# Fewer waits on VectorE, and sixteen partitions of one load moved to GpSimd's queue

## The chip, the cores and the metric

One core of a Trainium2 chip runs the kernel. The metric is the device time of one execution in microseconds (us), the median of several runs. Runs of the kernel before lie within 0.3% of each other in most rounds (172.23 to 172.75 us) and within 0.6% in the worst. All runs used here are marked fast. "Chain" below means the chain of work that ended last, followed back from the last instruction. The profile is one traced execution; its span is about 2 us shorter than the device time (170.5 against 172.72 before).

## The reference

```python
x = np.abs(np.random.randn(32, 512, 1024)).astype(np.float32) + 1e-6
return np.sum(1.0 / x, axis=-1).astype(np.float32)
```

That is 16,384 rows of 1024 numbers, 67.1 MB in, 64 KB out. With 128 partitions, each partition holds 128 consecutive rows.

## The kernel before

It takes 1/a + 1/b = (a + b)/(ab) for the two halves of a row, so one reciprocal serves two numbers. GpSimd multiplies the halves (some rows: TensorE copies a half to PSUM and VectorE multiplies). ScalarE makes exp(-ln(ab)). Then VectorE multiplies and sums. "A" rows multiply both halves by the reciprocal; the rows of "B" and "C" take a + b from TensorE, and a C chunk leaves one of its products to VectorE.

```python
A, B, C = (2, 0, 0), (2, 2, 0), (2, 2, 1)      # rows, sums by TensorE, products by VectorE
LOADS = [[A, B, A, C]] * 10 + [[A, B], [A, C]] * 4 + [[A], [B], [A], [C]] * 2
...
ring = opool.tile([P, R, D], f32)              # R = 40 rows per partition
...
    for j in range(e, m):
        row = xc[:, j, :].rearrange("p (h e) -> p h e", h=2)
        sum_row(c + j, row, rc[:, j - e, :].unsqueeze(1).to_broadcast([P, 2, H]))
    for j in range(e):
        sum_row(c + j, pr[:, j, :], sm[j])
...
for chunks in LOADS:
    n = sum(m for m, _, _ in chunks)
    xt = ring[:, c0 % R : c0 % R + n, :]
    keep(nc.sync.dma_start(out=xt, in_=x_v[:, c0 : c0 + n, :]))
```

There are 26 loads: ten of 8 rows (numbers 0 to 9), eight of 4 (10 to 17), eight of 2. Up to 40 rows stand in the ring, so SyncE queues loads some 37 us before they land.

## Time and profile before

| | before |
|---|---|
| device time | 172.72 us (172.23 to 172.75, 3 runs) |
| span of the profile | 170.5 us |
| busy: PE, VectorE, ScalarE, GpSimd | 80, 73, 78, 78% |
| DMA over the span | 394 GB/s, 9 tenths or more in 36 slices |
| last load: first and last of its 16 landings | 158.94 and 162.02 us |

How to read it: no compute engine is full, the DMA engines are. A load's semaphore (the counter on which engines wait) counts 16 landings; the profile's busy share of the 16 DMA engines is 1.00 to 1.01 from 13 to 158 us. I read the landings as one from each engine; no trace names the engine. The prediction works out from this what sets the end.

### The profile page before, as it was taken

To read this page: it belongs to the slowest core of one execution; us is meant where nothing else is said; L and a number is where in the kernel's file an instruction comes from. 1 tells how busy PE (TensorE), PEld (TensorE's weight loads), DVE (VectorE), ACT (ScalarE), POOL (GpSimd) and SP (SyncE) were. 2 spreads that over 40 slices of the span, in tenths; PEclk is the share of its full clock that TensorE was granted. 3 is DMA by queue.
4 is the path that set the end of the run, shared out by engine and by line. 5 is a ranking of instruction groups with operands and counts; after the bars stand their busy time and mean duration, and the time that the engine had idled before them with its cause. 6 is when DMAs were issued, how large, how long until landed. Compare 5 with 4: busy or idle time off the path is not lost.

```text
span 170.5 us, 1320 instructions
## 1 busy us (share of the span) xinstructions
PE 136.0 (80%) x288; PEld 52.7 (31%) x288; DVE 124.9 (73%) x272; ACT 133.5 (78%) x129; POOL 133.0 (78%) x70
## 2 busy tenths in 40 slices
PE   0008999988889888786988887979999998896790
PEld 0003444332332333242333323323434332332240
DVE  0001778777987777787777769888998988889683
ACT  3002979979787997959799797899999988999790
POOL 1008969696996969589696969999999799996930
PEclk9999999999999999999999999999999999999999
DMA  6999999999999999999999999999999999999300
GB/s 208 415 446 431 438 423 446 415 454 423 448 423 431 431 438 419 431 432 423 446 415 446 423 404 427 431 423 431 427 427 423 427 413 423 421 421 419 146 0 15
DMA packets 3895, 67.25 MB, mean 394 GB/s; under 512 B 432, under 2 KB 560, under 8 KB 560
## 3 DMA queue, kind: packets, MB, share of 16 engines
q1 hardware_dynamic: 3888, 67.18, 92.7%
q8 instruction: 2, 0.03, 0.1%
q14 instruction: 5, 0.04, 0.1%
HBM read 67.11 MB, written 0.07 MB: 394 GB/s over the span
## 4 chain that ended last, share of the span: by engine, by line
DMA 66%; POOL 23%; issue 6%; DVE 1%; ACT 1%; DVEq 0%; POOLq 0%
DMA ring<-in_x_dram 66%; POOL pr L136 23%; DVE ring L92 1%; ACT pr L147 1%; ACT rc L151 1%; DVE pr L92 0%; DVEq L190 0%; POOLq L136 0%; DVE sums L92 0%; DVEq L92 0%
## 5 line engine op out<-in xcount | busy, mean ns | idle before, releaser
L136 POOL TENSOR_TENSOR pr<-ring 128x1024 f32<-128x1024 f32 x64 | 132.3, 2099 | 29.9 <-DMA ring<-in_x_dram 29.7
L82 PE MATMUL s<-ring,ident 128*128 128x512 f32 x256 | 121.2, 612 | 14.7 <-DVE sums L92 13.0
L92 DVE CUSTOM_DVE_ANT_1 ring<-ring,rc 128x1024 f32<-128x1024 f32 x64 | 75.6, 1219 | 26.2 <-ACT rc L151 22.2
L147 ACT ACTIVATE pr<-pr 128x1024 f32<-128x1024 f32 x64 | 67.3, 1051 | 30.0 <-POOL pr L136 29.7
L82 PEld LDWEIGHTS s<-ring,ident 128*128 128x128 f32 x256 | 47.4, 193 | 86.6 <-issue 49.4
L92 DVE CUSTOM_DVE_ANT_0 pr<-pr,s 128x512 f32<-128x512 f32 x64 | 41.4, 683 | 0.8 <-ACT pr L157 0.7
L157 ACT ACTIVATE pr<-pr 128x1024 f32<-128x1024 f32 x32 | 33.8, 1057 | 1.0
L151 ACT ACTIVATE rc<-pr 128x1024 f32<-128x1024 f32 x32 | 32.9, 1028 | 1.0
L82 PE MATMUL b<-ring,ident 128*128 128x512 f32 x32 | 18.5, 662 | 16.0 <-DMA ring<-in_x_dram 15.8
L125 DVE TENSOR_TENSOR pr<-ring,b 128x512 f32<-128x512 f32 x16 | 10.9, 684 | 16.1 <-PE b L82 16.0
L82 PEld LDWEIGHTS b<-ring,ident 128*128 128x128 f32 x32 | 5.3, 196 | 26.6 <-issue 15.4
L92 DVE DVE_READ_ACCUMULATOR2_ANT sums<- 128x1 f32 x128 | 10.6, 83 | 0.0
L53 ACT ACT_TABLE_LOAD x1 | 1.3, 1283 | 0.7 <-PEq L179 0.7
masks.py:197 POOL MEMSET ident<- 128x128 f32 x1 | 0.2, 204 | 0.3 <-POOLq L179 0.3
masks.py:199 POOL TENSOR_SCALAR_AFFINE_SELECT ident<-ident 128x128 f32<-128x128 f32 x1 | 0.3, 292 | 0.1
L179 POOL MEMSET const-float32-0.0<- 128x1 f32 x1 | 0.1, 98 | 0.2 <-issue 0.2
L179 POOL MEMSET const-bfloat16-1.0<- 128x1 bf16 x1 | 0.1, 101 | 0.0
L179 POOL MEMSET const-uint8-127<- 128x1 uint8 x1 | 0.1, 101 | 0.0
L179 POOL MEMSET const-float32-1.0<- 128x1 f32 x1 | 0.1, 98 | 0.0
## 6 DMA issues: line engine op xcount, KB each, us to landing
ring<-in_x_dram SPq DMA_DIRECT2D x10, 4096.0 KB, 37.7
ring<-in_x_dram SPq DMA_DIRECT2D x8, 2048.0 KB, 36.7
ring<-in_x_dram SPq DMA_DIRECT2D x8, 1024.0 KB, 28.2
out_dram<-sums SPq DMA_DIRECT2D x1, 64.0 KB, 1.5
```

Source lines behind the costliest of these rows:

```text
L53: nc.scalar.add_instruction(mybir.InstLoadActFuncSet(name=nc.get_next_instruction_name(), act_func_set_id=act_sets.index("natural_log_exp_ ...
L82: i = nc.tensor.matmul(bank, lhsT=ident, rhs=half, start=k == 0, stop=k == len(halves) - 1,)
L92: i = nc.vector.tensor_tensor_reduce(out=row, in0=row, in1=fac, scale=S, scalar=0.0, op0=mult, op1=plus, accum_out=sums[:, c : c + 1],)
L125: i = nc.vector.tensor_tensor(out=pr[:, j, :], in0=xt[:, q + j, :H], in1=b, op=mult)
L136: i = nc.gpsimd.tensor_tensor(out=pr[:, v:, :], in0=xc[:, v:, :H], in1=xc[:, v:, H:], op=mult)
L147: keep(nc.scalar.activation(out=pr, in_=pr, func=Ln, scale=S))
L151: i = nc.scalar.activation(out=rc, in_=pr[:, e:, :], func=Exp, scale=-1.0)
L157: keep(nc.scalar.activation(out=r, in_=r, func=Exp, scale=-1.0))
L179: nc = _bacc.Bacc("TRN2", target_bir_lowering=False, num_devices=1)
```

## The change

The intent, as I read it from the diff: VectorE's program becomes shorter (separate semaphore waits go from 87 to 51, and five C chunks become B), and the 16 DMA engines are to end together: in load 10 (rows 80 to 83), 16 of the 128 partitions are taken from SyncE's transfer and given to GpSimd's queue, in two groups of eight, each behind a transfer of eight single elements. The diff, cut to its core:

```diff
+    UPPER, Q, AHEAD = 80, 112, 64
-    LOADS = [[A, B, A, C]] * 10 + ...
+    LOADS = [[A, B, A, B], [A, B, A, C]] * 5 + ...
-    ppool: bufs=6, one tag
+    ppool: bufs=4 for each of two tags, "ps" and "pr"
     # sum_rows
+                pr[:, e : e + 2, :] if j == e and m - e > 1 else None,   # output of an A chunk's first row
-        for j in range(e):
+        for j in reversed(range(e)):
     # loads
-        keep(nc.sync.dma_start(out=xt, in_=x_v[:, c0 : c0 + n, :]))
+        if c0 == AHEAD:
+            for p0 in range(Q, P, 8):
+                for w, rows in ((1, 1), (D, 4)):
+                    dst = spare if rows == 1 else ring
+                    r0 = 0 if rows == 1 else UPPER % R
+                    keep(nc.gpsimd.dma_start(
+                        out=dst[p0 : p0 + 8, r0 : r0 + rows, :w],
+                        in_=x_v[p0 : p0 + 8, UPPER : UPPER + rows, :w]))
+        h = Q if c0 == UPPER else P
+        keep(nc.sync.dma_start(out=xt[:h], in_=x_v[:h, c0 : c0 + n, :]))
```

(The two ppool lines are paraphrased.)

More of the change, by code (lines that the diff above doesn't have):

```diff
@@ L41 @@
     A, B, C = (2, 0, 0), (2, 2, 0), (2, 2, 1)
-    LOADS = [[A, B, A, C]] * 10 + [[A, B], [A, C]] * 4 + [[A], [B], [A], [C]] * 2
+    LOADS = [[A, B, A, B], [A, B, A, C]] * 5 + [[A, B], [A, C]] * 4 + [[A], [B], [A], [C]] * 2
     Ln = mybir.ActivationFunctionType.Ln
@@ L60 @@
     )
-    ppool = ctx.enter_context(tc.tile_pool(name="ppool", bufs=6))
+    ppool = ctx.enter_context(tc.tile_pool(name="ppool", bufs=4))
     opool = ctx.enter_context(tc.tile_pool(name="opool", bufs=1))
@@ L75 @@
     sums = opool.tile([P, F], f32)
+    spare = opool.tile([P, 1, 1], f32)
     ident = opool.tile([P, P], f32)
@@ L89, in add, with sum_row @@
             keep(i)
-    def sum_row(c, row, fac):
+    def sum_row(c, row, fac, out=None):
         i = nc.vector.tensor_tensor_reduce(
-            out=row,
+            out=row if out is None else out,
             in0=row,
@@ L107, in sum_rows @@
             row = xc[:, j, :].rearrange("p (h e) -> p h e", h=2)
-            sum_row(c + j, row, rc[:, j - e, :].unsqueeze(1).to_broadcast([P, 2, H]))
-        for j in range(e):
+            sum_row(
+                c + j,
+                row,
+                rc[:, j - e, :].unsqueeze(1).to_broadcast([P, 2, H]),
+                pr[:, e : e + 2, :] if j == e and m - e > 1 else None,
+            )
+        for j in reversed(range(e)):
             sum_row(c + j, pr[:, j, :], sm[j])
@@ L116 @@
         xt = ring[:, c0 % R : c0 % R + n, :]
-        keep(nc.sync.dma_start(out=xt, in_=x_v[:, c0 : c0 + n, :]))
+        if c0 == AHEAD:
[3 more added lines that the diff above has]
+                    r0 = 0 if rows == 1 else UPPER % R
+                    keep(
+                        nc.gpsimd.dma_start(
+                            out=dst[p0 : p0 + 8, r0 : r0 + rows, :w],
+                            in_=x_v[p0 : p0 + 8, UPPER : UPPER + rows, :w],
+                        )
+                    )
+        h = Q if c0 == UPPER else P
+        keep(nc.sync.dma_start(out=xt[:h], in_=x_v[:h, c0 : c0 + n, :]))
         made, q = [], 0
         for m, e, v in chunks:
-            pr = ppool.tile([P, m, H], f32, tag="pr")
+            pr = ppool.tile([P, m, H], f32, tag="ps" if e else "pr")
             for j in range(v):
```

## The prediction

The forecast's sum came to -0.9 - 0.5 - 0.05 = -1.45 us, and the reason for the -0.5 us (on which engines the rows of load 10 land) is an assumption that was not shown. Without that term the sum is -0.95 us, 171.8 us. The sign "within 1.7 us" leans on the same term. Cut as well are an allowance for GpSimd's issues, which counted 0 us, and a fourth case: that the transfers of load 10 themselves run slowly, at 173.5 to 176 us, with the chance of 0.15 that is missing from the list; the 0.03 for over 2% slower is its worst part.

> **What bounds the kernel now.** I read first the slices of the page, because they show whether one resource is busy from end to end.
>
> ```profile
> DMA  6999999999999999999999999999999999999300
> GB/s 208 415 446 431 438 423 446 415 454 423 448 423 431 431 438 419 431 432 423 446 415 446 423 404 427 431 423 431 427 427 423 427 413 423 421 421 419 146 0 15
> q1 hardware_dynamic: 3888, 67.18, 92.7%
> q8 instruction: 2, 0.03, 0.1%
> q14 instruction: 5, 0.04, 0.1%
> ```
>
> The 16 DMA engines are full from the first slice to slice 37 and then stop. No compute engine is over 80% (PE 80, GpSimd and ScalarE 78, VectorE 73), so the middle of the kernel is a stream of 67.1 MB. The records of single packets give the rate: a row of 32 KB takes 1.213 us on its engine (27.0 GB/s), one of 16 KB 0.614 us, one of 8 KB 0.313 us. Each engine carries 1/16 = 4.19 MB, 155.3 us at that rate. It starts at 1.75 us, so an engine with nothing else to do would end near 157 to 158 us.
>
> Next the busy time by stretches, to see how the stream ends (us, then PE, PEld, DVE, ACT, POOL, clock, DMA share, GB/s):
>
> ```profile
> 156.00:158.00 2.00, 0.78 (x2) 0.49 (x3) 1.93 (x6) 1.97 (x3) 0.97 (x2) 1.00 1.01 422
> 158.00:159.00 1.00, 1.00 (x3) 0.38 (x2) 0.27 (x1) 0.60 (x1) 1.00 (x1) 1.00 0.77 320
> 159.00:160.00 1.00, 1.00 (x4) 0.51 (x3) 1.00 (x3) 0.35 (x1) 0.92 (x2) 1.00 0.24 98
> 160.00:161.00 1.00, 0.89 (x3) 0.06 (x1) 1.00 (x1) 0.97 (x2) 1.00 (x1) 1.00 0.16 66
> 161.00:162.00 1.00, 0.00 (x0) 0.00 (x0) 0.28 (x3) 0.79 (x1) 1.00 (x1) 1.00 0.02 8
> ```
>
> Most engines are done at 160 us; a few run on to 162. The semaphore of each load records 16 landings[...]. In the last load they lie at 0 to 1.00 us after the first for 13 engines, and at 2.17, 2.18 and 3.08 for three. The load is usable only at the last, 162.02 us. In the first load all 16 lie within 0.89 us, so the lag grows on the way, in steps: one engine 0.29 further at load 4, one to 2.15 at load 6, one to 2.2 at load 10, one to 2.17 at load 16, and one from 2.19 to 3.09 at load 23.
>
> These steps follow the instruction packets of q8 and q14, the only other traffic. Their records stand at 46.25, 73.07, 105.51, 106.37 and 154.09 us (8 KB each) and 64.89 and 131.32 (16 KB). Beside each, one data packet is too long: at 154.41 an 8 KB row took 0.968 us in place of 0.313. So the fetch at 154.09 costs its engine 0.327 + 0.655 = 0.98 us. I counted instructions in the trace: VectorE had started 69, 199 and 325 by 46.25, 105.51 and 154.09, steps of about 128. I read these three as VectorE's fetches, all on one DMA engine: 3 x 0.97 over a starting offset of 0.2 gives the 3.09 of the last engine.
>
> Last, the chain that ended last:
>
> ```profile
> 131.56 25.52 DMA ring<-in_x_dram
> 157.08 0.02 issue
> 157.11 0.04 POOLq L136
> 157.15 0.09 issue
> 157.24 2.36 POOL pr L136
> 159.60 0.09 issue
> 159.69 2.38 POOL pr L136
> 162.07 0.02 issue
> 162.09 1.07 ACT pr L147
> 163.16 0.02 issue
> 163.18 1.04 ACT rc L151
> ```
>
> Load 23's slowest landing (157.08) releases GpSimd, then come GpSimd's product for load 24 (which itself landed at 159.56), ScalarE, VectorE, and the store: 13.4 us from that landing to the end at 170.5. The end moves with the slowest DMA engine of the last three loads.
>
> [...]
>
> **The change, part by part.**
>
> *VectorE's program.* Three edits cut it: the first row of an A chunk writes to pr, the two rows of B and C are taken in reverse, and the tiles are split over two tags with four buffers each. From the built programs: VectorE has 364 instructions before and 323 after; 36 of the 41 are separate semaphore waits (87 to 51), 5 are products. The third fetch came at about the 325th traced instruction (327th of the program with its two branches). 323 stays below that, by four, so this fetch should not happen. The slowest engine then ends at 3.09 - 0.95 = about 2.15, beside the other two at 2.17 and 2.18: -0.9 us. The waits themselves are worth little: they lie beside the stream, and in the tail I see 0.04 + 0.09 us between ScalarE's end and the first VectorE row. I put 0.05 down for it.
>
> *Five C chunks become B.* Five VectorE products at 0.684 us (3.4 us) and ten TensorE passes go; GpSimd gains 5 half products of about 1 us. A load takes 9.71 us to arrive and costs GpSimd 7.4 us before, 8.4 in the five new ones. Both fit: 0 us.
>
> *Load 10 (rows 80 to 83).* SyncE's part has 112 partitions: 16 engines with 7 rows of 16 KB in place of 8, each 0.61 us less. The two GpSimd groups have 8 rows each. [...]
>
> *GpSimd's issues.* No duration of one is in this trace[...]. GpSimd has 2.3 us spare per load, and loads stand 36.5 us in the queue at the median, so no transfer should start late. 0 us.
>
> Sum if all works: -0.9 - 0.5 - 0.05 = -1.45 us, and 172.72 - 1.45 = 171.3 us. The tail moves as a whole, because load 22 (153.70) falls back by the 0.6 us that GpSimd needs to be free in time.
>
> **Rivals.**
>
> *Only the fetch counts.* [...] the move helps some and loads others: the last engine ends at 2.18 to 2.79 and the gain is 0.3 to 0.9 us, 171.8 to 172.4. For it: the trace names no engine.
>
> [...]
>
> *The fetch still comes*, if my boundary is off by four instructions or GpSimd's longer program (123 to 137) crosses one of its own: the -0.9 falls away and 172.1 to 172.7 remains. GpSimd fetched once, at its 68th; its next would be at about 196. Against.
>
> **Range and chances.** I give the full sum 0.55, the fetch alone 0.2, no gain 0.1[...]. The centre lies a little above the full sum: 171.5 us, range 170.7 to 173.6. Over 2% faster would be under 169.3 us, which needs 3.4 us from a spread of 3.1: 0.02. Over 2% slower is above 176.2[...]: 0.03. Within 2%: 0.95.
>
> **What would show it.** Right: four 8 KB instruction packets on q14 in place of five, none near 154 us; the last load's landings within 1.7 us; last landing near 160.5; the tail after load 23's landing still about 13.4 us. Wrong: long data packets between 95 and 120 us[...], a landing spread still above 2 us[...], a fifth packet (boundary), or SyncE's loads issued so late that DMA slices fall below 9.

## The result, and the profile after

The changed kernel takes 181.01 us (180.38 to 181.47, 4 runs) against 172.55 us for the kernel before beside it: ratio 1.049, 95% interval 1.045 to 1.053. It is slower by 8.5 us, where 171.5 was predicted. A ratio here is the mean time of one kernel's fast runs over that of the other's of the same rounds, so it is not quite the ratio of the medians.

The slices and queues of the changed kernel (each digit or number is 1/40 of the span, here 4.49 us):

```profile
DMA  6999999999999999999999899999999999999300
GB/s 219 438 424 438 438 438 409 453 431 402 440 446 424 424 453 427 418 431 438 416 431 415 194 161 234 299 431 422 431 427 427 427 414 418 425 418 425 166 0 15
q1 hardware_dynamic: 3872, 66.91, 92.0%
q0 software_dynamic: 128, 0.26, 0.9%
q8 instruction: 2, 0.03, 0.1%
q14 instruction: 4, 0.03, 0.0%
```

Two things are to be seen. The row of busy shares looks the same as before, one 8 among the nines: in the slow slices packets of 32 KB were open for up to 3.3 us in place of 1.21, and as I read it an engine counts as busy while a packet is open. The GB/s row beneath it does not: four slices show 194, 161, 234 and 299 in place of some 427. That is 233 + 266 + 193 + 128 = 820 GB/s missing, times 4.49 us 3.7 MB, or 8.6 us of the full rate: the whole loss. And q14 has four instruction packets in place of five, as predicted.

Stretches of the changed kernel (us, then PE, PEld, VectorE, ScalarE, GpSimd busy, granted clock, DMA share, GB/s):

```profile
95.00:98.00 3.00, 2.84 (x7) 1.40 (x8) 0.79 (x5) 2.08 (x2) 3.00 (x2) 1.00 1.10 418
98.00:102.00 4.00, 1.85 (x5) 0.53 (x4) 3.57 (x8) 3.67 (x4) 4.00 (x3) 0.96 0.91 180
...
104.00:108.00 4.00, 0.91 (x2) 0.50 (x2) 0.93 (x2) 0.88 (x1) 0.64 (x1) 0.50 0.98 156
108.00:112.00 4.00, 4.00 (x6) 1.65 (x5) 2.01 (x6) 2.08 (x2) 4.00 (x3) 0.51 1.03 238
112.00:115.00 3.00, 3.00 (x8) 1.32 (x8) 3.00 (x7) 2.71 (x3) 3.00 (x3) 1.00 0.93 229
115.00:118.00 3.00, 3.00 (x8) 1.33 (x8) 2.02 (x5) 2.94 (x4) 2.87 (x2) 1.00 1.01 431
```

The rate falls at 98 us, when GpSimd's first eight rows of 16 KB move (their packets start at 98.06 to 98.40, with one at 100.56), again with the second eight (104.25 to 107.65), and is back at 115 us, when load 10 and its neighbours are through. In between, 32 KB packets took up to 3.3 us in place of 1.21, GpSimd's sixteen rows 0.71 to 2.32 us, and most other 16 KB packets about 1.1 us, up to 2.6, in place of 0.614. TensorE's granted clock falls to 0.5 here too; it is not needed for the loss: the run with two halves below loses 6.5 us with a mean clock of 1.000.

The chain of the changed kernel, near its end:

```profile
135.94 27.02 DMA ring<-in_x_dram
...
163.08 2.37 POOL pr L157
...
165.60 2.35 POOL pr L157
...
168.05 2.38 POOL pr L157
170.43 0.02 issue
170.46 1.06 ACT pr L168
171.52 0.02 issue
171.55 1.04 ACT rc L172
```

The tail is nearly that of before. Here three products of GpSimd follow the landing of load 22 without a gap; before, GpSimd stood idle for 1.03 us in between, until load 23 landed (157.08). From the landing of load 22 (162.95) to the end are 16.6 us; before it was 153.70 to 170.5, 16.8 us. From the landing of load 23 (165.44), the sign that the prediction names, it is 14.0 us in place of 13.4. From the last landing of the last load to the landing of the output it is 7.66 us in place of 7.47, so only 0.2 us was lost there. The first landing of the last load moved from 158.94 to 167.25 and the last from 162.02 to 170.36. Note the first one: the DMA engine that fared best lost 8.3 us. No engine escaped. (Loads were queued long before, 38 us in the median, so late issue is no explanation.)

### The profile page after: what moved, and what is told of

It reads as the page before. It is cut to its first block, busy times and chain, and to the rows that moved or that the text cites. A ratio compares the mean times of both kernels' runs of the same rounds, so it can differ in the third digit from the quotient of the medians.

```text
span 179.5 us, 1277 instructions
## 1 busy us (share of the span) xinstructions
PE 137.3 (76%) x278; PEld 52.4 (29%) x278; DVE 122.5 (68%) x267; ACT 134.3 (75%) x129; POOL 140.6 (78%) x74
## 4 chain that ended last, share of the span: by engine, by line
DMA 79%; POOL 11%; DVE 3%; ACT 2%; issue 2%; SPq 0%; POOLq 0%; DVEq 0%
DMA ring<-in_x_dram 79%; POOL pr L157 11%; DVE pr L95 2%; DVE ring L95 1%; ACT pr L168 1%; ACT rc L172 1%; SPq L138 0%; POOLq L157 0%; DVE sums L95 0%; DVEq L95 0%; DVEq L211 0%
## 5 line engine op out<-in xcount | busy, mean ns | idle before, releaser
L157 POOL TENSOR_TENSOR pr<-ring 128x1024 f32<-128x1024 f32 x64 | 137.7, 2180 | 30.6 <-DMA ring<-in_x_dram 28.0
L85 PE MATMUL s<-ring,ident 128*128 128x512 f32 x256 | 126.4, 634 | 31.9 <-DVE sums L95 15.9
L85 PEld LDWEIGHTS s<-ring,ident 128*128 128x128 f32 x256 | 48.4, 198 | 106.6 <-issue 65.5
L95 DVE CUSTOM_DVE_ANT_1 pr<-ring,rc 128x1024 f32<-128x1024 f32 x32 | 39.1, 1221 | 48.4 <-ACT rc L172 48.2
L95 DVE CUSTOM_DVE_ANT_1 ring<-ring,rc 128x1024 f32<-128x1024 f32 x32 | 38.9, 1217 | 0.0
L85 PE MATMUL b<-ring,ident 128*128 128x512 f32 x22 | 13.3, 687 | 5.8 <-DMA ring<-in_x_dram 5.5
L146 DVE TENSOR_TENSOR pr<-ring,b 128x512 f32<-128x512 f32 x11 | 7.5, 684 | 5.2 <-PE b L85 5.1
L85 PEld LDWEIGHTS b<-ring,ident 128*128 128x128 f32 x22 | 4.0, 213 | 15.1 <-DMA ring<-in_x_dram 13.9
L132 POOL DMA_DIRECT2D spare<-in_x_dram x2 | 1.2, 610 | 0.0
L132 POOL DMA_DIRECT2D ring<-in_x_dram x2 | 1.0, 521 | 0.0
```

The source lines that it names most:

```text
L85: i = nc.tensor.matmul(bank, lhsT=ident, rhs=half, start=k == 0, stop=k == len(halves) - 1,)
L95: i = nc.vector.tensor_tensor_reduce(out=row if out is None else out, in0=row, in1=fac, scale=S, scalar=0.0, op0=mult, op1=plus, accum_out ...
L132: nc.gpsimd.dma_start(out=dst[p0 : p0 + 8, r0 : r0 + rows, :w], in_=x_v[p0 : p0 + 8, UPPER : UPPER + rows, :w],)
L146: i = nc.vector.tensor_tensor(out=pr[:, j, :], in0=xt[:, q + j, :H], in1=b, op=mult)
L157: i = nc.gpsimd.tensor_tensor(out=pr[:, v:, :], in0=xc[:, v:, :H], in1=xc[:, v:, H:], op=mult)
```

## The experiments

What I set out to test after this: that the transfers of load 10 slow all 16 DMA engines while they move, by the partitions of SBUF (the on-chip memory) that they write. (How the partitions would do that was an assumption of mine; no run shows it.) Rivals: the edits to VectorE and to the buffers cost part of it; GpSimd's queue is the cause (its packets, its descriptors, the single elements); the addresses in HBM are the cause. Each kernel ran beside the kernel before on the same chip. The edits are to the kernel before unless said otherwise; `extra` is a tile of 4 rows that nothing reads, so transfers into it add bytes and touch no result. All gave correct results. The diffs are cut to the lines that matter; comments in them, and lines that are not code, are mine.

**e1: the VectorE edits alone.**

```diff
# from the changed kernel: GpSimd's transfers out, load 10 whole again
-        if c0 == AHEAD: ...
-        h = Q if c0 == UPPER else P
-        keep(nc.sync.dma_start(out=xt[:h], in_=x_v[:h, c0 : c0 + n, :]))
+        keep(nc.sync.dma_start(out=xt, in_=x_v[:, c0 : c0 + n, :]))
```

> The changed kernel without its GpSimd transfers and with the whole 128-partition load 10: all VectorE edits, none of the split. Theory (the third VectorE fetch is gone and the split alone costs): four 8 KB instruction packets, none near 154 us, the last landing of the last load 0.9 us earlier (near 161.1 us), time 171.3 to 171.9 us, ratio 0.994 to 0.997. Rival (the edits to VectorE and to the buffers cost part of the 8.5 us): above 173 us.

171.86 us (171.81 to 172.06, 5 runs) against 172.29: ratio 0.9976, interval 0.9964 to 0.9989. So these edits cost nothing; they gain 0.4 us, far under 2% but clear of the noise of these rounds, and this version is the fastest of the three. Its queue line, and the stretches at the end of its stream:

```profile
q14 instruction: 4, 0.03, 0.0%
```

```profile
159.00:160.00 1.00, 1.00 (x4) 0.22 (x2) 1.00 (x3) 0.96 (x1) 0.90 (x2) 1.00 0.24 98
160.00:161.00 1.00, 0.29 (x1) 0.00 (x0) 1.00 (x3) 0.97 (x2) 1.00 (x1) 1.00 0.14 57
161.00:162.00 1.00, 0.54 (x2) 0.30 (x3) 0.99 (x5) 0.67 (x2) 0.90 (x2) 1.00 0.00 0
```

Four instruction packets, at 47.53, 75.48, 106.36 and 117.81 us, none near 154; the last landing is at 161.42 (before 162.02), 2.33 us after the first (before 3.08). As predicted, one packet is gone and the last landing is earlier. Of its 0.6 us not all reaches the end, as the chain of this kernel shows:

```profile
161.46 1.12 PE b L85 x2
162.59 3.45 PE s L85 x8
...
166.20 0.69 DVE pr L95
```

The last chunk's rows are now taken in reverse, so VectorE's first row there needs TensorE's last sum (166.04). The output's landing moves from 169.49 to 169.07, 0.42 us.

**e2: the split alone.**

```diff
# GpSimd's four transfers and the 112-partition load 10, in the kernel before
```

> The kernel before with the split of load 10 alone (112 partitions by SyncE, two groups of eight by GpSimd, each behind eight single elements). Theory (the split costs all of it): the fetch at 154 us stays, so about 9.4 us more than before, 181 to 183 us, DMA rate down to 150 to 300 GB/s between about 97 and 115 us. Rival (the split costs only together with the new order and buffers): under 178 us.

181.99 us (181.15 to 183.09) against 172.29, +9.7. The split alone costs more than the whole change did (8.5 us). With the 0.4 us that e1 gains, the sum would be 9.3; the 0.8 us between that and 8.5 no run explains. The fifth instruction packet is there again (164.0 us).

**e3: load 10 as 112 and 16 partitions, both by SyncE.**

```diff
+        if c0 == UPPER:
+            keep(nc.sync.dma_start(out=xt[:112], in_=x_v[:112, c0 : c0 + n, :]))
+            keep(nc.sync.dma_start(out=xt[112:], in_=x_v[112:, c0 : c0 + n, :]))
```

> The kernel before with load 10 as two transfers of SyncE, partitions 0 to 111 and 112 to 127; nothing on GpSimd. Theory[...]: 16 KB rows at 1.1 us in place of 0.614 for the 112 part (7 x 0.5 = 3.4 us)[...]: 4 to 6.5 us more, 176.5 to 179. Rival (GpSimd's queue is the cause, its interleaving or its small packets): within 0.6 us of before, under 173.2.

179.22 us (178.02 to 179.33), +6.9, with nothing on GpSimd: its queue is not needed for the loss. More than I expected, and the range holds a term for the 16 partitions: the 3.4 us are for the 112 alone.

**e4: GpSimd's groups into the extra tile, load 10 whole.**

```diff
+        if c0 == AHEAD:
+            for p0 in (112, 120):
+                for w, rows in ((1, 1), (D, 4)):
+                    dst = spare if rows == 1 else extra
+                    keep(nc.gpsimd.dma_start(
+                        out=dst[p0 : p0 + 8, :rows, :w],
+                        in_=x_v[p0 : p0 + 8, UPPER : UPPER + rows, :w]))
```

> The kernel before, whole 128-partition load 10, and GpSimd's two groups of eight partitions (112 to 119, 120 to 127) with their single elements as well, written to an extra tile that nothing reads: 0.26 MB more (0.6 us if spread evenly). Theory[...]: two stalls of about 2 us, 3 to 5 us more, 175.5 to 177.5, 32 KB packets of 2 to 3 us near 95 to 108 us. Rival (the 112-partition load is the whole cost): 0.6 to 1.2 us more, under 174.

179.26 us (178.56 to 179.78), +7.0. GpSimd's groups cost by themselves, with load 10 whole. Both e3 and e4 lie above my upper figure.

**e5 and e9: two halves against odd and even.**

```diff
# halves
+            keep(nc.sync.dma_start(out=xt[:64], in_=x_v[:64, c0 : c0 + n, :]))
+            keep(nc.sync.dma_start(out=xt[64:], in_=x_v[64:, c0 : c0 + n, :]))
# odd and even
+            for s in range(2):
+                keep(nc.sync.dma_start(out=xt[s:P:2], in_=x_v[s:P:2, c0 : c0 + n, :]))
```

> The kernel before with load 10 as two transfers of SyncE, partitions 0 to 63 and 64 to 127, so 16 engines with 4 rows each, twice. [...] Theory[...]: 4 to 6 us more, 176.5 to 178.5. Rival (what costs is 7 rows per engine, or 112 not being a power of two): within 0.6 us of before.

> As the two halves, but the even partitions in one transfer and the odd ones in the other[...]. Theory[...]: clearly less than the halves, 0 to 3 us more, 172.3 to 175.5. Rival (any transfer that is not the 128-partition one [...]pays the same): as the halves, 176.5 or more.

The halves: 178.79 us (178.39 to 179.56), +6.5. Odd and even: 172.81 us (172.62 to 173.18) against 172.33, +0.5. Same bytes, same queue, two transfers of 64 partitions in both, with 16 landings for each, as I read the pages (448 and 449 packets under 512 B against 432 before, where the kernel has as many landings). First the GB/s row of the halves, then that of odd and even:

```profile
GB/s 207 422 437 444 415 444 444 415 444 444 409 437 437 430 419 444 432 422 444 422 430 430 319 207 206 313 430 430 426 430 419 433 415 419 424 426 413 206 0 15
```

```profile
GB/s 207 415 445 422 445 415 453 415 461 407 455 422 430 430 430 434 422 447 422 438 422 438 422 403 426 430 430 430 430 430 415 426 409 422 424 424 415 131 0 15
```

While the halves move, the rate is 206 to 207 GB/s, half of the usual 430. With the odd and even partitions the row shows no dent: between 99 and 105 us no row of 16 KB took more than 0.62 us there, while in the halves most took 1.1 to 1.3 us. So it is neither the number of transfers nor rows per engine: it is which partitions one transfer covers.

**e6: GpSimd's groups on every fourth partition in place of eight neighbours (edit to e4).**

```diff
-            for p0 in (112, 120):          # partitions p0 .. p0 + 7
+            for p0 in (64, 65):            # partitions p0, p0 + 4, ... p0 + 28
```

> As e4_groups_extra (GpSimd's two groups of eight into an extra tile, whole load 10), but the eight partitions of a group are 64, 68, ... 92 and 65, 69, ... 93[...]. Same bytes, same queue, same small transfers. Theory[...]: most of the 7 us goes, 0.5 to 2 us more than before, 173 to 174.5. Rival (GpSimd's queue, its packets or its descriptors stall the engines): as e4, 178 to 180.

176.29 us (175.92 to 176.69), +4.0: 3 us less than in e4, but twice what I had expected. That was left open here, and two runs below take it up.

**e7: the groups by SyncE (edit to e4).**

```diff
-            nc.gpsimd.dma_start(...)  with the single elements
+            nc.sync.dma_start(...)    without them, between loads 7 and 8
```

> The two groups of eight partitions (112 to 119, 120 to 127) into the extra tile, issued by SyncE between loads 7 and 8, without GpSimd and without the small transfers; whole load 10. Theory ([...]whichever queue): 4 to 8 us more, 176.5 to 180. Rival (GpSimd's queue): 0.6 to 1.5 us more, 173 to 174.

178.70 us (178.61 to 178.86), +6.4, against +7.0 from GpSimd. Most of it is not GpSimd's.

**e10 and e11: source or destination (edits to e4).**

```diff
# e10: source rows of 112..127, destination partitions 64, 68, ... 93
# e11: source rows of 64, 68, ... 93, destination partitions 112..127
```

> As e4_groups_extra, but each group reads rows of partitions 112 to 119 (120 to 127) of the input and writes them to partitions 64, 68, ... 92 (65, 69, ... 93) of the extra tile: the source of e4, the destination of e6. Theory (the SBUF side decides): as e6, 175.5 to 177. Rival (the addresses in HBM decide): as e4, 178.5 to 180.

> The opposite pairing: rows of partitions 64, 68, ... 92 of the input go to partitions 112 to 119 of the extra tile. Theory (the SBUF side decides): as e4, 178.5 to 180. Rival (HBM addresses): as e6, 175.5 to 177.

e10: 176.36 us (175.99 to 177.00), as e6 (176.29). e11: 178.77 us (178.73 to 179.54), as e4 (179.26) within half a microsecond. The destination in SBUF decides; the HBM addresses do not.

**e8: e4 without the single elements.**

```diff
-                for w, rows in ((1, 1), (D, 4)):
+                for w, rows in ((D, 4),):
```

> As e4_groups_extra without the single elements[...]. Theory[...]: the same as e4, 178 to 180. Rival (the single elements[...] cost): at least 2 us less, under 177.3.

179.06 us (178.34 to 180.03), as with them. The single elements make no difference here. What they are for, and on which engines the groups fell, no trace shows.

**e14 and e15: every fourth partition, in the lower and in the upper half.**

```diff
# e14: SyncE, partitions 0, 4, ... 28 and 1, 5, ... 29
# e15: SyncE, partitions 64, 68, ... 92 and 65, 69, ... 93
```

> As e7_sync_groups (two groups of eight rows of 16 KB by SyncE between loads 7 and 8, extra tile), but partitions 0, 4, ... 28 and 1, 5, ... 29. [...] Theory[...]: 1.2 us at most, 172.3 to 173.9. Rival (any small transfer in the stream, or one on half the engines, stalls it): 175 or more.

> As e14_sync_own, but partitions 64, 68, ... 92 and 65, 69, ... 93[...]. Theory[...]: as e6 and e10, 175 to 177.5. Rival ([...]GpSimd's queue made the 3.9 us of e6): as e14, under 174.

e14: 173.63 us (173.46 to 173.90) against 172.30, +1.3. e15: 175.96 us (175.62 to 176.08), +3.7. The same stretches in three kernels show it: first e14 (every fourth partition from 0 and from 1), then e15 (from 64 and from 65), then e7 (112 to 119 and 120 to 127).

```profile
80.00:82.00 2.00, 0.99 (x3) 0.51 (x4) 1.57 (x6) 1.78 (x3) 1.57 (x2) 1.00 1.07 459
82.00:84.00 2.00, 2.00 (x6) 0.76 (x5) 1.36 (x3) 1.97 (x3) 0.95 (x1) 1.00 1.03 442
```

```profile
80.00:82.00 2.00, 1.11 (x3) 0.64 (x4) 1.44 (x6) 1.77 (x3) 1.45 (x2) 1.00 1.10 262
82.00:84.00 2.00, 0.87 (x3) 0.04 (x1) 1.48 (x3) 1.97 (x3) 0.00 (x0) 1.00 0.98 246
```

```profile
80.00:82.00 2.00, 1.16 (x3) 0.68 (x4) 1.40 (x6) 1.79 (x3) 1.40 (x2) 1.00 1.57 197
82.00:84.00 2.00, 0.83 (x2) 0.00 (x0) 1.55 (x3) 1.97 (x3) 0.00 (x0) 1.00 0.73 107
```

In e14 the rate stays full, 459 and 442 GB/s, and the 1.3 us fit two rows of 0.61 us on one engine (an estimate: each of these transfers has eight landings, by the 448 packets under 512 B against 432; that both fall on the same eight engines is not shown). In e15 the rate falls to 262 and 246 GB/s, in e7 to 197 and 107. The landings of the last load say the same: the first came at 159.30 us in e14, 0.36 us later than before, but at 161.26 in e15, 2.3 us later. So the engine that fared best lost almost nothing in e14, and in e15 even that one was held back. This answers e6: rows on every fourth partition of the upper half cost 3.7 us from SyncE too, against 4.0 from GpSimd, so GpSimd's queue is not needed for it.

Why these partitions cost and those of e14 do not is not shown. e14 and e15 differ in nothing but the partitions (0 to 29 against 64 to 93), and by e10 and e11 it is the written ones that count. Whether the half decides, or the engine from which a row comes, no run tells apart. And in e9, where I had allowed 0 to 3 us, no row was slowed at all.

**e13: the 16 partitions alone.**

```diff
+            keep(nc.sync.dma_start(out=extra[112:], in_=x_v[112:, UPPER : UPPER + 4, :]))
```

> Whole load 10, and partitions 112 to 127 (four rows) once more by SyncE between loads 7 and 8 into the extra tile: one row on each of 16 engines[...]. It is the second transfer of e3 by itself. Theory: [...] 2 to 4.5 us more, 174.5 to 177; the rest of e3's 6.9 us is then the 112-partition transfer. Rival (the 112 part is harmless): 6 us or more, 178.3 or above.

176.85 us (176.40 to 177.08), +4.55, at the top of the range. By subtraction, as an estimate, 6.93 - 4.55 = 2.4 us of e3 belong to the 112-partition transfer. With the groups' 7.0 us of e4 that makes 9.4, near the 9.7 us of the split alone, if the parts simply add.

**e12: the last chunk forward again (from e1).**

```diff
-        for j in reversed(range(e)):
+        for j in range(e) if c + m == F else reversed(range(e)):
```

> e1_vector_only with the two rows of the very last chunk in forward order again. In e1 VectorE waits at the end for TensorE's last sum (166.04 us), because row 1 comes first. Theory: 0.1 to 0.4 us less than e1, 171.4 to 171.8, ratio to before 0.995 to 0.997. Rival (the added second wait costs as much): as e1, 171.9.

172.31 us (171.65 to 172.81, 6 runs) against 172.48 in its rounds, ratio 0.9983, interval 0.9960 to 1.0006. By time it is not told apart from e1, nor clearly from before. The profiles, one execution each, do show the point: from the last landing of the last load to the landing of the output it is 7.47 us before, 7.65 in e1 and 7.43 in e12. So the reversed order costs some 0.2 us at the very end.

## Why the prediction was wrong

**What bounds the kernel:** right. The end followed the DMA engines and the tail kept its length to within 0.6 us (14.0 against 13.4 us from load 23).

**VectorE's program:** the direction was right, the size was off. The packet near 154 us, which I read as VectorE's third fetch, is gone in the changed kernel and in e1 (four packets in place of five). That reading rests on counts (69, 199 and 325 instructions started); no record names the engine that a packet serves. "-0.9 us" measured 0.6 us at the last landing: the spread shrank by 0.75, and the first landing was 0.15 later. At the end 0.4 was left, because the reversed order, which I had booked as a gain, put TensorE's last sum on the path (0.2 us, by the profiles of e1 and e12). Four further fetches in e1, as I read the counts two of VectorE and two of TensorE, still hold three engines back by 2.0 to 2.3 us.

**Five C chunks become B, and GpSimd's issues:** no cost was seen; e1 with all of the former is faster than before. The four issues took 0.52 to 0.70 us, 2.3 us together, less than I had allowed (that figure came from no trace).

**Load 10:** here the prediction failed. I wrote that the engines get "7 rows of 16 KB in place of 8, each 0.61 us less", and counted 0.61 us for every row of the groups. (SyncE's part did have 16 landings, 111.50 to 115.58 us.) The cost of a row was what failed: 0.61 us is its time in a 128-partition load, and I carried it over to transfers of another shape. In the changed kernel GpSimd's rows took 0.71 to 2.32 us, most other 16 KB rows between 98 and 114 us about 1.1, and 32 KB rows of other loads up to 3.3. In place of -0.5 us the split cost 9.7 us by itself (e2).

**The rival** that the transfers of load 10 themselves run slowly: its sign, long data packets between 95 and 120 us, is what the profile shows; but I gave it 0.15 and a wrong size. It took the stall as a matter of one half of the engines, which the lag of 2 us would partly hide. The runs show all 16 landings later: the best engine lost 8.3 us in the changed kernel, and in e7 4.3 us (first landing of the last load 163.27 against 158.94). So there is no fast half in which to hide it. And I held against it that the bytes stay the same in total, which was no argument: e9 and e5 move the same bytes to the same partitions and differ by 6 us. What counts, as measured, is which partitions one transfer covers.

**Rivals that fell:** the fetch at the boundary did not return. That the slow engines lie in the wrong half could not be seen under 8 us of stall. Whether a move of rows between engines can pay at all stays open. It seems doubtful: sixteen rows in small transfers cost 3.7 us in e15 and 7.0 in e4, more than the lag of 2 to 3 us that they were to remove; only in e14 did they cost less, 1.3 us. In all three they were extra rows, not moved ones: this is argued, not tried.

**Not settled:** why the written partitions matter, and why all 16 landings of later loads come late. The trace records packets, not the paths that they take.

## What to carry to other kernels

Keep a load whole, over 128 partitions: in that shape the loads ran at some 427 GB/s here. Sixteen rows sent to eight neighbouring partitions at a time, or to every fourth partition of the upper half, slowed all engines here by 3.7 to 7 us, and the busy share does not show it, only the GB/s row does. Not every other shape costs as much: the odd and even partitions cost 0.5 us, and e14 1.3 us, about the time of its rows. Compare the first landing of a load as well as its last: if even the first is late, as in e15 by 2.3 us and in the changed kernel by 8.3, every engine waited, and balancing between engines is not the remedy. VectorE's shorter program (36 separate waits fewer) left four instruction packets in place of five, and e1 with it gained 0.4 us of 172.
